# Twelve places for raw weight units, four for split halves, and another order of experts in a one-core decoder layer

## The chip, the core and the metric

The kernel runs on one core of a Trainium2 chip. All times are microseconds (us) on the device. The metric is the time of one execution. Before the change three runs took 1787.58, 1795.78 and 1796.42 us (median 1795.78). Another execution was taken by the hardware profiler: 1789.81 us, of which 1788.0 us lie between its first and its last instruction. All times inside the program are read from that execution, counted from the start of this span.

The engines are named as in the profile: PE is the matrix engine (PEld its weight loads), DVE the vector engine, ACT the scalar engine, POOL the general engine. SP only issues DMAs here; its queue is in order, so a DMA that waits holds back every DMA behind it.

## The reference

One decoder layer on 512 tokens of 1024 channels. The first part (a projection that feeds a causal convolution branch and an mLSTM branch, gates, output projection, layer norm) is not touched by the change. The second part is a mixture of 32 experts of which each token uses four:

```
logits = x2d @ router_w + router_b
top_logit, top_idx = lax.top_k(logits, TOP_K)      # 4 of 32
gate = jax.nn.softmax(top_logit)
...                                                # per expert, on its tokens
h = x[tok] @ w1[e] + b1[e]                         # 1024 -> 2048
g, lin = split(h); g = min(g, 7); lin = clip(lin, -7, 7)
act = g * sigmoid(1.702 * g) * (lin + 1)
y = act @ w2[e] + b2[e]                            # 1024 -> 1024
acc[tok] += w * y
x = layer_norm(ALPHA * x + acc)
```

All weights are 32-bit floats: an expert has 8 MiB of w1 and 4 MiB of w2, 384 MiB in all.

## The kernel before, in words

**Units.** The expert weights lie in memory in *units* of 1 MiB (128 partitions of 2048 floats): eight of w1 and four of w2 for an expert, 384 units in all. `Units.fetch` (line 250) takes the next place of a rotating list, one 8 KiB column of on-chip memory over all partitions, and issues one DMA into it on SP. A place is free again when the last instruction that reads its unit has run. The list (line 1300) has eight places: one of `raw2`, two of `raw`, three of `raw3`, and two of the pool `hl3`, which `Other` lends out as raw places.

**Split or plain.** Experts are ranked by how many tokens they have, and the rank fixes the shape (`RANKS`, line 282): the rows of a block are 128, 64 or 32. Blocks of 64 and 32 rows multiply with the raw unit in plain 32-bit (line 388). Blocks of 128 rows use units that are split into a high and a low half-precision part: `split` (line 270) makes of each half of a unit an ACT copy (line 273) and a DVE subtraction (line 276), into one of six places (two of `hl2`, four of `hl`), and PE runs three passes over them (line 400).

**Kinds of expert.** In the order string `TURNS` (line 293) a letter is a kind: `l` one block of 64 rows, `s` one of 32, `n` 64 and 32, `m` one of 128, `h` 128 and 64 for ranks 1 to 3, and in the kernel before also rank 0, which has two blocks of 128. In front of the string stands `FIRST`, the expert number 0, a block of 128.

**Order of work.** `moe` (line 306) goes through the experts. For the i-th it runs `gemm1` on half 0 of w1 (four units), the first two w2 units of the expert before (`gemm2`), `gemm1` on half 1 (four units), then the last two w2 units of the expert before, and `send` adds the result to the sum `ysum` in memory. So a *block* of work is eight w1 units of expert i and four w2 units of expert i-1. Fetches are issued in this order, as far as places allow. Eight w1 units of `FIRST` are fetched ahead (`ahead`, line 1301). The instruction order on each engine is fixed when the program is built.

**The output biases.** `bias2` (line 1314) adds the gated b2 rows to the token sums `xt` and stores those to `ysum`. It is called at the end of round 0. For each of four token tiles it adds two gate tables, transposes 32 columns, copies, multiplies (line 1332) and adds to `xt`, one tile after the other through a single small buffer. `xt` is the tile `hT` of the profile; after these stores its 16 KiB per partition lie unused until the end, when line 533 loads `ysum` back into it.

Of the kernel before, what the change touches and what calls it, by code (L numbers as in the profile page):

```python
# [23 lines left out]
def f32(ap):  # L24
    return ap.bitcast(F32)
# [74 lines left out]
class Router:  # L100
# [3 lines left out]
    def __init__(self, nc, cp, wp, c, rw, gate, perm):  # L104
        self.nc, self.c, self.rw = nc, c, rw
        self.gate, self.perm = gate, perm

        self.pos1 = cp.tile([P, NT, E], F32, name="pos1")
        self.vals = cp.tile([P, NT, E, 4], F32R, name="vals")
        self.sel = cp.tile([P, E], F32, name="selc")  # L110
        self.selh = cp.tile([P, E], BF, name="selh")
        self.cnt = cp.tile([P, E], F32, name="cnt")
        self.sj = wp.tile([P, NT, TOPK, E], F32, name="sj")
        self.selb = wp.tile([P, NT, 3, E], BF, name="selb")
        self.permf = cp.tile([P, E], F32, name="permf")
# [126 lines left out]
class Units:  # L242


    def __init__(self, nc, raw, hl, pool_share=POOL_HALVES):
        self.nc, self.raws, self.hls = nc, raw, hl
        self.share = pool_share
        self.n = self.f = 0

    def fetch(self, src):  # L250
        w = self.raws[self.f % len(self.raws)].tile([P, 2048], F32, name="raw")
        self.f += 1
        self.nc.sync.dma_start(w, src)
        return w

# [34 lines left out]
    return [(sum(rows[:b]), rows[b]) for b in range(len(rows))]  # L290


TURNS = "lhslmnlhslmlnhslslnmlhslnmlnsll"


def turns():

    kinds = dict(h=[1, 2, 0, 3], m=list(range(4, 8)), n=list(range(8, 13)), l=list(range(13, 25)), s=list(range(25, 31)))
    return [FIRST] + [kinds[k].pop(0) for k in TURNS]


def unit(w, e, *at):
    return w[(e, *at)] if isinstance(e, int) else w[(bass.ds(e, 1), *at)].rearrange("o p n -> p (o n)")


def moe(tc, units, ahead, wr, wq, pp, ph, c, R, x1d, ysum, acc, w1, w2, B1, xg, early, bias2, last, xs, ne=E):

# [72 lines left out]
    def product(xs, outs, w, u, first, end):  # L380

        for x, o in zip(xs, outs):
            if x.dtype == F32:
                m = x.shape[2]
                d = width(m)
                for k in range(2):
                    for j in range(P // m):
                        nc.tensor.matmul(o[j * m:(j + 1) * m], x[:, 2 * u + k, :],  # L388
                                         w[:, k * 1024 + j * d:k * 1024 + (j + 1) * d],
                                         start=first and k == 0, stop=end and k == 1)  # L390
        if all(x.dtype == F32 for x in xs):
# [36 lines left out]
    def swiglu(h, act, half, to):  # L428

        n = act.shape[1]  # L430
        gm = wq.tile([P, F], F32, name="gm", bufs=1)[:, 0:n]
        if half == 0:
            sg = wq.tile([P, F], F32, name="sg", bufs=1)[:, 0:n]
            nc.vector.tensor_scalar(gm, h, LIMIT, None, op0=OP.min)  # L434
            nc.scalar.activation(sg, gm, AF.Sigmoid, scale=SW_ALPHA)  # L435
            nc.vector.scalar_tensor_tensor(act, gm, to[0][:, 0:1], sg, op0=OP.mult, op1=OP.mult)
        else:
            nc.vector.tensor_scalar(gm, h, LIMIT, -LIMIT, op0=OP.min, op1=OP.max)  # L438
            nc.vector.scalar_tensor_tensor(act, gm, 1.0, act, op0=OP.add, op1=OP.mult)
# [8 lines left out]
    def gemm2(ev, half, hs, ys):  # L448

        for u in range(2 * half, 2 * half + 2):  # L450
            product(hs, ys, units.fetch(unit(w2, ev, u)), u, u == 0, u == 3)

    def send(ys, tos):

# [24 lines left out]
    nc.vector.tensor_copy(R.perm, R.permf[0:1])  # L479
    pend = None  # L480
    for i, r in enumerate(seq):
        ev = 0 if r == FIRST else nc.sync.value_load(R.perm[0:1, r:r + 1], min_val=0, max_val=ne - 1)
        more = i + 1 < E
        if i == 0:
            gt, oh = gather(seq[1], 0, False)
            x1 = rows(oh)
            gts = [gather(r, 0, False)[0]]
            for t in range(NT):
                nc.scalar.activation(acc[:, t, :], acc[:, t, :], AF.Copy, scale=ALPHA)
        elif more:  # L490
            gt, g = gather(seq[i + 1], 0)
        acts = [width(m) for m in RANKS[r]]
        if acts[0] == F:
            acts = [wq.tile([P, F], F32, name="act", bufs=2)[:, 0:d] for d in acts]
        else:
            act = wq.tile([P, F], F32, name="act", bufs=2)
            acts = [act[:, i * 512:i * 512 + d] for i, d in enumerate(acts)]
        hold = {}
        for h, act, to in zip(gemm1(r, ev, 0, xs, hold), acts, gts):
            swiglu(h, act, 0, to)  # L500
        if pend is not None:
            pe, pa, pg = pend
# [12 lines left out]
        if pend is not None:
            gemm2(pe, 1, hs, ys)
            if more:
                send(ys, pg)
            else:
                final = [keep(ys[0], pg[0][0])]  # L520
        if i == 0:
            bias2()
        if i == 1:
            early()
        pend = (ev, acts, gts)
        if more:
            gts = gtn
# [685 lines left out]
        return f32(self.pool.tile([P, 2, 1024], F32R, name="hl")).rearrange("p a b -> p (a b)")  # L1213


def body(tc, I, out, ne=E):
    nc = tc.nc
    top = ExitStack()
# [78 lines left out]
        nc.vector.tensor_sub(xs[:, 1, part, :], rows0[g], f32(xs[:, 0, part, :]))  # L1297
    R.order(wp6, pm)

    units = Units(nc, [raw2, raw, raw, raw3, raw3, raw3, Other(hl3), Other(hl3)], [hl2] * 2 + [hl] * 4, set())  # L1300
    ahead = deque(units.fetch(unit(w1, 0, i // 4, i % 4)) for i in range(8))
    nc.scalar.dma_start(posd, R.pos1)
    nc.scalar.dma_start(vald, f32(R.vals))
    nc.gpsimd.memset(xg, 0.0)
# [8 lines left out]

    def bias2():

        b2 = wl.tile([P, D], F32, name="act", bufs=2)[0:E]
        nc.sync.dma_start(b2, I["b2"])
        for n in range(2):
            cols = slice(n * 512, (n + 1) * 512)
            ps = pm.tile([P, 512], F32, name="tp", bufs=2)[0:E]  # L1320
            nc.tensor.matmul(ps, R.sel[0:E, :], b2[:, cols], start=True, stop=True)
            nc.scalar.copy(b2[:, cols], ps)
        for t in range(NT):
            w = wl.tile([P, T], F32, name="gm", bufs=1)
            nc.vector.tensor_add(w[:, 0:E], f32(R.vals[:, t, :, 1]), f32(R.vals[:, t, :, 2]))
            tp = pm.tile([P, 4, P], F32, name="tp", bufs=2)
            nc.tensor.transpose(tp[0:E, 0, :], w[:, 0:E], c["ident"])
            wT = w[0:E, P:2 * P]
            nc.scalar.copy(wT, tp[0:E, 0, :])
            for n in range(2):  # L1330
                ps = pm.tile([P, 512], F32, name="tp", bufs=2)
                nc.tensor.matmul(ps, wT, b2[:, n * 512:(n + 1) * 512], start=True, stop=True)  # L1332
                x = xt[:, t, n * 512:(n + 1) * 512]
                nc.vector.tensor_add(x, ps, x)
# [24 lines left out]
        nc.vector.scalar_tensor_tensor(o, o, r, b, op0=OP.mult, op1=OP.add)  # L1359
        nc.sync.dma_start(out[t * P:(t + 1) * P, :], o)  # L1360

    moe(tc, units, ahead, wr, wl, pm, ph, c, R, x1d, ysum, xt, w1, w2, B1, xg, early, bias2, last, [xs], ne)
    mo.close()

    again = nc.values_load(tabs[0:1, 3, 0:1], min_val=0, max_val=1)
# [41 lines left out]
```

## Time and profile before

| | us |
|---|---|
| median of three runs | 1795.78 |
| the profiled execution | 1789.81 |
| its span | 1788.0 |
| expert stage, from PE's first product of `FIRST` to the last weight unit | 601.7 to about 1745 |
| tail: last sums, layer norm, output | 1743 to 1788 |

PE is busy for 1650.9 us (92%), but a matmul's end is modelled and a wait inside a stretch of short matmuls hardly shows as idle time. The DMA engines' busy share is high in most of the expert stage and falls in a few places; these are in the rows below.

### The profile page before, as it was taken

Reading aid. Unit: us, or ns where it says so; the run is one execution under the profiler, and the core shown is the slowest. Engines: PE = TensorE matmul, PEld = TensorE weight load, DVE = VectorE, ACT = ScalarE, POOL = GpSimd, SP = SyncE. Lnnn points to the kernel's source line nnn. Section 1 sums busy time; section 2 is a strip of 40 time slices with the busy share of each in tenths; the row PEclk is TensorE's granted clock in tenths of the full one; section 3 lists DMA queues with packets and bytes.
Section 4 is the critical chain, followed back from the end, with each engine's and each line's share of the span. In section 5 each row is a group of like instructions: output and inputs, shape, how many; then the busy total and the mean of one; then the engine's idle time right before and its main releaser. Section 6 shows DMA issues by size and latency. Waiting matters only on the chain.

```text
span 1788.0 us, 22808 instructions
## 1 busy us (share of the span) xinstructions
PE 1650.9 (92%) x8848; PEld 1001.8 (56%) x8864; DVE 952.9 (53%) x1423; ACT 554.0 (31%) x731; POOL 228.3 (13%) x169
## 2 busy tenths in 40 slices
PE   7999999899999989989999899998799998999874
PEld 5778878688878836545455453763235553453321
DVE  5999998967567846335353343541125541342013
ACT  4442353434343424223242332421023430231001
POOL 0110031014212001010010301001010102010100
PEclk9999999899999879999999999998999999999997
DMA  5222222122244656999989999689999889999992
GB/s 193 94 71 89 89 94 71 47 95 95 95 157 186 285 205 231 345 394 415 395 327 369 401 414 408 247 315 395 413 412 410 330 325 403 410 408 389 400 419 92
DMA packets 77282, 488.63 MB, mean 273 GB/s; under 512 B 9792, under 2 KB 11600, under 8 KB 22290
## 3 DMA queue, kind: packets, MB, share of 16 engines
q1 hardware_dynamic: 65762, 460.90, 64.5%
q0 software_dynamic: 8960, 19.39, 4.7%
q10 hardware_dynamic: 2448, 6.84, 1.0%
q8 instruction: 71, 1.16, 0.3%
q14 instruction: 41, 0.34, 0.1%
HBM read 471.18 MB, written 19.07 MB: 274 GB/s over the span
## 4 chain that ended last, share of the span: by engine, by line
PE 76%; DMA 13%; DVE 6%; ACT 2%; issue 1%; POOL 0%; SPq 0%; ACTq 0%; DVEq 0%
PE h L388 18%; PE mm L759 18%; PE h L400 13%; DMA raw<-w 10%; PE y L388 7%; PE mm L656 6%; PE y L400 6%; DVE hl L276 2%; DVE acc L816 1%; DMA hT<-ysum 1%; PE tp L366 1%; PE sc L919 1%; PE tp L375 1%; PE h L420 1%; PE tp L1332 1%
## 5 line engine op out<-in xcount | busy, mean ns | idle before, releaser
L276 DVE TENSOR_TENSOR hl<-raw,hl 128x1024 fp32r<-128x1024 f32 x261 | 322.9, 1265 | 130.9 <-ACT hl L273 129.4
L273 ACT CAST hl<-raw 128x1024 fp32r<-128x1024 f32 x261 | 265.0, 1048 | 211.1 <-PE mm L759 75.7
L388 PE MATMUL h<-raw,xs 128*32 128x256 f32 (+1 forms) x2016 | 299.2, 499 | 25.6 <-DMA raw<-w 25.4
L759 PE MATMUL mm<-xhl,hl 128*128 128x512 f32 x1176 | 291.1, 402 | 8.7 <-ACT hl L273 8.7
L400 PE MATMUL h<-hl,xs 128*128 128x512 f32 x1008 | 252.0, 403 | 14.4 <-ACT hl L273 10.0
L759 PEld LDWEIGHTS mm<-xhl,hl 128*128 128x128 f32 x1176 | 224.1, 191 | 64.4 <-ACT hl L273 9.4
L400 PEld LDWEIGHTS h<-hl,xs 128*128 128x128 f32 x1008 | 188.4, 191 | 79.0 <-ACT hl L273 16.1
L388 PEld LDWEIGHTS h<-raw,xs 128*32 128x32 f32 (+1 forms) x2016 | 94.0, 125 | 195.1 <-issue 133.2
L816 DVE SCALAR_TENSOR_TENSOR acc<-zp,vec,acc 128x512 f32<-128x512 f32 x240 | 182.9, 775 | 2.0
L438 DVE TENSOR_SCALAR gm<-h 128x512 f32<-128x512 f32 (+2 forms) x41 | 30.7, 749 | 221.6 <-PE h L388 155.4
L388 PE MATMUL y<-raw,hs 128*64 128x512 f32 (+1 forms) x832 | 128.4, 500 | 6.1 <-DMA raw<-w 4.1
L434 DVE TENSOR_SCALAR gm<-h 128x512 f32<-128x512 f32 (+2 forms) x41 | 30.7, 748 | 193.0 <-PE h L388 161.8
L342 POOL DMA_INDIRECT xg<-x1d,idx x39 | 57.3, 1469 | 540.0 <-DVE oh L325 296.3
L460 POOL DMA_INDIRECT ysum<-yo,idx x39 | 64.6, 1657 | 451.3 <-ACT yo L459 342.3
L400 PE MATMUL y<-hl,hs 128*128 128x512 f32 x432 | 115.1, 410 | 5.6 <-DVE hl L276 2.9
L388 PE MATMUL h<-hl,xs 128*32 128x256 f32 (+1 forms) x672 | 101.0, 492 | 3.6 <-DMA hl<-w 3.3
L400 PEld LDWEIGHTS y<-hl,hs 128*128 128x128 f32 x432 | 78.3, 190 | 37.7 <-issue 10.1
L656 PE MATMUL mm<-hl,xhl 128*128 128x512 f32 x384 | 94.5, 398 | 1.7 <-ACT sg L809 1.5
L388 PEld LDWEIGHTS y<-raw,hs 128*64 128x64 f32 (+1 forms) x832 | 38.5, 124 | 77.8 <-issue 60.0
L656 PEld LDWEIGHTS mm<-hl,xhl 128*128 128x128 f32 x384 | 71.5, 188 | 18.6 <-ACT sg L809 1.8
L459 ACT COPY yo<-y 128x512 f32<-128x512 f32 (+2 forms) x35 | 21.5, 629 | 191.7 <-PE y L388 143.5
L435 ACT ACTIVATE sg<-gm 128x512 f32<-128x512 f32 (+2 forms) x41 | 27.8, 678 | 151.4 <-DVE gm L434 151.3
(308 smaller groups left out, 1576.3 us busy)
## 6 DMA issues: line engine op xcount, KB each, us to landing
raw<-w SPq DMA_DIRECT2D x288, 1024.0 KB, 12.2
hl<-w SPq DMA_DIRECT2D x96, 1024.0 KB, 11.3
raw<-wf SPq DMA_DIRECT2D x44, 1024.0 KB, 4.8
cvp<-xT SPq DMA_DIRECT2D x8, 256.0 KB, 5.4
hT<-x SPq DMA_DIRECT2D x1, 2048.0 KB
x1d<-hT ACTq DMA_DIRECT2D x4, 512.0 KB, 6.3
ysum<-hT ACTq DMA_DIRECT2D x4, 512.0 KB, 2.6
hT<-ysum SPq DMA_DIRECT2D x1, 2048.0 KB, 22.4
```

Source lines behind the costliest of these rows:

```text
L273: nc.scalar.copy(s[:, 0, :], w)
L276: eng.tensor_sub(s[:, 1, :], w, f32(s[:, 0, :]))
L342: nc.gpsimd.indirect_dma_start(out=g, out_offset=None, in_=split_rows(x1d, m), in_offset=bass.IndirectOffsetOnAxis(ap=ix[:, 0:1], axis=0), ...
L388: nc.tensor.matmul(o[j * m:(j + 1) * m], x[:, 2 * u + k, :], w[:, k * 1024 + j * d:k * 1024 + (j + 1) * d], start=first and k == 0, stop=e ...
L400: nc.tensor.matmul(o[:, j, :], x[:, a, 2 * u + k, :], s[k][:, b, j * 512:(j + 1) * 512], start=first and k == 0 and i == 0, stop=end and k ...
L434: nc.vector.tensor_scalar(gm, h, LIMIT, None, op0=OP.min)
L435: nc.scalar.activation(sg, gm, AF.Sigmoid, scale=SW_ALPHA)
L438: nc.vector.tensor_scalar(gm, h, LIMIT, -LIMIT, op0=OP.min, op1=OP.max)
L460: nc.gpsimd.indirect_dma_start(out=split_rows(ysum, P * d // D), out_offset=bass.IndirectOffsetOnAxis(ap=ix[:, 0:1], axis=0), in_=o, in_of ...
L656: nc.tensor.matmul(ps, src[:, a, kk, t * P:(t + 1) * P], w[k][:, b, :], start=(kk == 0 and (a, b) == PASS[0]), stop=(kk == KD - 1 and (a, ...
L759: nc.tensor.matmul(ps, w[k][:, a, j * P:(j + 1) * P], mov[:, b, k, :], start=(k == 0 and (a, b) == PASS[0]), stop=(k == KD - 1 and (a, b) ...
L816: nc.vector.scalar_tensor_tensor(o, z[:, j:j + T], V("dw_w", m * CT + j), o, op0=OP.mult, op1=OP.add)
```

## The change

Five edits:

- The places for raw units are ten from the start: `raw2`, two of `raw`, three of `raw3`, two of `hl3`, two of `hl2`. Once `bias2` has stored `xt`, the method `also` adds its two 8 KiB slices in front of the list: twelve. Before round 30 (`i == E - 2`) the slices are taken out again, since `xt` is loaded at the end.
- The split halves have four places (`hl`) instead of six.
- Two w2 units of `FIRST` are fetched ahead with its eight w1 units (`ahead2`).
- `bias2` runs between the two halves of round 0's first-layer work and the next expert, and its products run on four groups of 32 rows: one transpose for all four token tiles, and the four tiles' products each on its own group of rows and into its own bank.
- The order string is another, and rank 0 has a letter of its own, `H`.

```diff
-        self.nc, self.raws, self.hls = nc, raw, hl
+        self.nc, self.raws, self.hls = nc, deque(raw), hl
...
+    def also(self, places):
+        self.raws.extend(p for p in places)
+        self.raws.rotate(len(places))
+        self.raws = deque(p for p in self.raws if not isinstance(p, Slice) or p in places)
...
-        w = self.raws[self.f % len(self.raws)].tile([P, 2048], F32, name="raw")
-        self.f += 1
+        w = self.raws[0].tile([P, 2048], F32, name="raw")
+        self.raws.rotate(-1)
...
-TURNS = "lhslmnlhslmlnhslslnmlhslnmlnsll"
+TURNS = "lnllmlshlsHslmshlllnlmnnnmshsll"
...
-            product(hs, ys, units.fetch(unit(w2, ev, u)), u, u == 0, u == 3)
+            w = ahead2.popleft() if ahead2 else units.fetch(unit(w2, ev, u))
+            product(hs, ys, w, u, u == 0, u == 3)
...
+        if i == E - 2:
+            units.also([])
...
+        if i == 0:
+            bias2()
         if pend is not None:
...
-        if i == 0:
-            bias2()
...
+class Slice:
+    def __init__(self, ap):
+        self.ap = ap
+    def tile(self, *_, **__):
+        return self.ap
...
-    units = Units(nc, [raw2, raw, raw, raw3, raw3, raw3, Other(hl3), Other(hl3)], [hl2] * 2 + [hl] * 4, set())
+    units = Units(nc, [raw2, raw, raw] + [raw3] * 3 + [Other(hl3)] * 2 + [Other(hl2)] * 2, [hl] * 4, set())
     ahead = deque(units.fetch(unit(w1, 0, i // 4, i % 4)) for i in range(8))
+    ahead2 = deque(units.fetch(unit(w2, 0, i)) for i in range(2))
...
+        for n in range(2):
+            cols = slice(n * 512, (n + 1) * 512)
+            y = pm.tile([P, 2, 512], F32, name="y", bufs=1)
+            sums = [y[:, 0, :], y[:, 1, :]] + [pm.tile([P, 512], F32, name="tp", bufs=2) for _ in range(2)]
+            for t in range(NT):
+                part = slice(t * E, (t + 1) * E)
+                nc.tensor.matmul(sums[t], wT[part], p2[part, cols], start=True, stop=True)
+            for t in range(NT):
+                nc.vector.tensor_add(xt[:, t, cols], sums[t], xt[:, t, cols])
         for t in range(NT):
...
             nc.scalar.dma_start(ysum[t * P:(t + 1) * P], xt[:, t, :])
+        units.also([Slice(xt[:, 2 * k:2 * k + 2, :].rearrange("p a b -> p (a b)")) for k in range(2)])
```

The instruction order moves at three places. First, SP's queue where the expert stage begins; `raw<-w` and `hl<-w` are fetches, `TENSOR_LOAD perm` reads an expert's number, of which there are 31. Before:

```order
L253 DMA raw<-w 128x2048
L253 DMA hl<-w 128x2048 x2
L253 DMA raw<-w 128x2048 x3
L482 TENSOR_LOAD perm
L482 ISA x2
L253 ISA
L253 DMA raw<-w 128x2048
```

After, at the same place:

```order
L259 DMA raw<-w 128x2048
L259 DMA hl<-w 128x2048 x4
L259 DMA raw<-w 128x2048 x3
L491 TENSOR_LOAD perm
L491 ISA x2
```

Two more fetches stand ahead of the expert numbers. The fetches that before stood between the numbers are gone from there. SP's queue goes on, after the last two numbers, with the first fetches into `xt` (`hT<-w`):

```order
L491 TENSOR_LOAD perm
L491 ISA x2
L259 DMA hl<-w 128x2048
L259 ISA
L259 DMA hT<-w 128x2048
L259 ISA
L259 DMA hT<-w 128x2048
L259 ISA
```

Behind these two stand all the next fetches into the six `raw` places, which in the kernel before were issued as each came free.

Second, PE around `bias2`; L1321 and L1344 gather the b2 rows by rank, L1327 and L1350 transpose the gates, L1332 and L1359 are the products, L400 and L406 the split products of `FIRST`. Before:

```order
L420 LDWEIGHTS selh
L420 MATMUL h<-B_3618,selh 128x512
L1321 MATMUL tp<-act,selc 32x512 x2
L1327 MATMUL tp<-ident,gm 32x128
L1332 MATMUL tp<-act,gm 128x512 x2
L1327 MATMUL tp<-ident,gm 32x128
L1332 MATMUL tp<-act,gm 128x512 x2
```

After:

```order
L406 MATMUL h<-hl,xs 128x512 x12
L1344 MATMUL tp<-yo,gm 128x512 x2
L1350 MATMUL tp<-ident,gm 128x128
L1359 MATMUL y<-yo,gm 128x512 x2
L1359 MATMUL tp<-yo,gm 128x512 x2
L1359 MATMUL y<-yo,gm 128x512 x2
L1359 MATMUL tp<-yo,gm 128x512 x2
L336 MATMUL tp<-vals,oh 128x4 x4
```

It now follows the last product of `FIRST`'s first layer directly, with one transpose instead of four, while before the first half of the next expert's w1 came ahead of it.

Third, PE where rank 0 begins. The rows `y<-` are the w2 products of the expert before it, with the rows of that expert's blocks (64x512, 32x256). Before:

```order
L388 MATMUL y<-raw,hs_7524 64x512 x4
L400 MATMUL h<-hl,xs 128x512 x26
L375 MATMUL tp<-ident,xg 128x128 x8
L400 MATMUL h<-hl,xs 128x512 x14
L330 MATMUL tp<-vals,oh 128x4 x4
L400 MATMUL h<-hl,xs 128x512 x56
L366 MATMUL tp<-ident,act 128x128 x6
```

After:

```order
L394 MATMUL y<-hl,hs_6538 64x512 x8
L381 MATMUL tp<-ident,xg 128x128 x8
L336 MATMUL tp<-vals,oh 128x4 x4
L406 MATMUL h<-hl,xs 128x512 x24
L381 MATMUL tp<-ident,xg 128x128 x8
L406 MATMUL h<-hl,xs 128x512 x4
L336 MATMUL tp<-vals,oh 128x4 x4
L406 MATMUL h<-hl,xs 128x512 x20
L372 MATMUL tp<-ident,act 128x128 x2
L406 MATMUL h<-hl,xs 128x512 x48
L394 MATMUL y<-raw,hs_6836 32x256 x16
```

Rank 0 now stands between two `s` experts, whose w2 products (32x256) lie in its first layer; before, it followed an `n` expert.

## Rows read from the trace of the kernel before

**Rows 1.** The page: engines, and the span in 40 slices.

```profile
PE 1650.9 (92%) x8848; PEld 1001.8 (56%) x8864; DVE 952.9 (53%) x1423; ACT 554.0 (31%) x731; POOL 228.3 (13%) x169
PEclk9999999899999879999999999998999999999997
DMA  5222222122244656999989999689999889999992
```

**Rows 2.** Stretches: length, busy us of each engine, granted clock, DMA share, GB/s.

```profile
602.00:650.00 48.00, 45.30 (x222) 30.07 (x222) 30.44 (x43) 24.80 (x27) 0.00 (x0) 0.95 0.80 316
650.00:720.00 70.00, 65.81 (x254) 36.86 (x256) 44.11 (x71) 26.21 (x32) 6.77 (x13) 0.84 0.57 187
920.00:945.00 25.00, 25.00 (x113) 13.34 (x114) 11.28 (x13) 7.04 (x9) 1.95 (x2) 1.00 0.61 219
1120.00:1180.00 60.00, 60.00 (x362) 42.34 (x366) 33.32 (x38) 21.01 (x25) 3.08 (x3) 1.00 0.57 222
1405.00:1460.00 55.00, 54.93 (x311) 29.65 (x310) 31.75 (x35) 21.60 (x26) 6.48 (x4) 1.00 0.76 276
1460.00:1743.00 283.00, 250.66 (x1643) 107.17 (x1642) 74.00 (x123) 51.48 (x74) 30.81 (x20) 0.99 1.02 405
1743.00:1788.00 45.00, 20.60 (x64) 6.70 (x60) 16.02 (x24) 4.54 (x5) 2.22 (x4) 0.78 0.24 94
```

**Rows 3.** What SP's queue waited for: total us, times, longest.

```profile
SPq L253 <- DVE hl L276: 598.6, 99, 31.8
SPq L253 <- PE h L388: 474.5, 193, 29.0
```

**Rows 4.** DMA issues between 720 and 1743: count, size, median us to landing.

```profile
raw<-w SPq DMA_DIRECT2D x263, 1024.0 KB, 13.3
hl<-w SPq DMA_DIRECT2D x88, 1024.0 KB, 13.0
```

**Rows 5.** PE in order of time (start, us): four, two and four units' products.

```profile
692.04 11.32 PE L400 MATMUL h<-hl,xs 128*128 128x512 f32 x48
704.71 3.65 PE L388 MATMUL h<-raw,xs 128*64 128x512 f32 x16
740.15 3.63 PE L388 MATMUL h<-raw,xs 128*32 128x256 f32 x64
```

**Rows 6.** PE at the starts of blocks 5, 8, 14 and 16.

```profile
799.46 11.90 PE L400 MATMUL h<-hl,xs 128*128 128x512 f32 x38 [3.14 <-ACT hl L273]
904.75 0.70 PE L400 MATMUL h<-hl,xs 128*128 128x512 f32 x2
...
1116.84 0.74 PE L400 MATMUL h<-hl,xs 128*128 128x512 f32 x2 [1.63 <-ACT hl L273]
1210.10 0.50 PE L330 MATMUL tp<-vals,oh 128*128 128x4 f32 x4
```

**Rows 7.** The end of `FIRST`'s first layer, and the output biases.

```profile
629.70 2.56 PE L400 MATMUL h<-hl,xs 128*128 128x512 f32 x10
643.52 2.30 PE L1321 MATMUL tp<-act,selc 32*32 32x512 f32 x4 [2.20 <-DMA act<-b]
663.07 3.78 PE L1332 MATMUL tp<-act,gm 32*128 32x512 f32 x4 [0.40 <-ACT gm L1329]
666.88 0.69 DVE L1334 TENSOR_TENSOR hT<-tp,hT 128x512 f32<-128x512 f32 x1 [1.01 <-PE tp L1332]
```

**Rows 8.** Stores to `ysum` (median us to landing), and the reads of the expert numbers.

```profile
ysum<-hT ACTq DMA_DIRECT2D x4, 512.0 KB, 2.6
...
L482 SPq TENSOR_LOAD <-perm x31: 260/269/466, 603.5 to 626.3; - x31
```

**Rows 9.** What the split's ACT copy (L273) waited for between 602 and 1743.

```profile
  DMA raw<-w: 71.1, 24
  PE h L400: 28.5, 36
```

**Rows 10.** The page: the split's two instructions, count, busy us, mean ns.

```profile
L276 DVE TENSOR_TENSOR hl<-raw,hl 128x1024 fp32r<-128x1024 f32 x261 | 322.9, 1265 | 130.9 <-ACT hl L273 129.4
L273 ACT CAST hl<-raw 128x1024 fp32r<-128x1024 f32 x261 | 265.0, 1048 | 211.1 <-PE mm L759 75.7
```

More of the change, by code (lines that the diff above doesn't have):

```diff
@@ L245, in __init__ @@
     def __init__(self, nc, raw, hl, pool_share=POOL_HALVES):
-        self.nc, self.raws, self.hls = nc, raw, hl
+        self.nc, self.raws, self.hls = nc, deque(raw), hl
         self.share = pool_share
-        self.n = self.f = 0
+        self.n = 0
+    def also(self, places):
+        self.raws.extend(p for p in places)
+        self.raws.rotate(len(places))
+        self.raws = deque(p for p in self.raws if not isinstance(p, Slice) or p in places)
     def fetch(self, src):
-        w = self.raws[self.f % len(self.raws)].tile([P, 2048], F32, name="raw")
-        self.f += 1
+        w = self.raws[0].tile([P, 2048], F32, name="raw")
+        self.raws.rotate(-1)
         self.nc.sync.dma_start(w, src)
@@ L290, in blocks @@
     return [(sum(rows[:b]), rows[b]) for b in range(len(rows))]
-TURNS = "lhslmnlhslmlnhslslnmlhslnmlnsll"
+TURNS = "lnllmlshlsHslmshlllnlmnnnmshsll"
 def turns():
-    kinds = dict(h=[1, 2, 0, 3], m=list(range(4, 8)), n=list(range(8, 13)), l=list(range(13, 25)), s=list(range(25, 31)))
+    kinds = dict(h=[1, 2, 3], m=list(range(4, 8)), n=list(range(8, 13)), l=list(range(13, 25)), s=list(range(25, 31)), H=[0])
     return [FIRST] + [kinds[k].pop(0) for k in TURNS]
@@ L303, in unit, with moe @@
     return w[(e, *at)] if isinstance(e, int) else w[(bass.ds(e, 1), *at)].rearrange("o p n -> p (o n)")
-def moe(tc, units, ahead, wr, wq, pp, ph, c, R, x1d, ysum, acc, w1, w2, B1, xg, early, bias2, last, xs, ne=E):
+def moe(tc, units, ahead, ahead2, wr, wq, pp, ph, c, R, x1d, ysum, acc, w1, w2, B1, xg, early, bias2, last, xs, ne=E):
     nc = tc.nc
@@ L1314, in bias2 @@
     def bias2():
-        b2 = wl.tile([P, D], F32, name="act", bufs=2)[0:E]
-        nc.sync.dma_start(b2, I["b2"])
+        b2, p2 = (wl.tile([P, D], F32, name="yo", bufs=2) for _ in range(2))
+        nc.sync.dma_start(b2[0:E], I["b2"])
+        w = wl.tile([P, F], F32, name="gm", bufs=1)
+        sel = w[0:E, 2 * P:3 * P]
+        nc.vector.tensor_copy(sel.rearrange("p (t e) -> p t e", t=NT), R.sel[0:E, None, :].to_broadcast([E, NT, E]))
         for n in range(2):
             cols = slice(n * 512, (n + 1) * 512)
-            ps = pm.tile([P, 512], F32, name="tp", bufs=2)[0:E]
-            nc.tensor.matmul(ps, R.sel[0:E, :], b2[:, cols], start=True, stop=True)
-            nc.scalar.copy(b2[:, cols], ps)
@@ L1323, in bias2 @@
-        for t in range(NT):
[L1324 to L1334, printed above, removed]
+            ps = pm.tile([P, 512], F32, name="tp", bufs=2)
@@ new lines, in bias2 @@
+            nc.tensor.matmul(ps, sel, b2[0:E, cols], start=True, stop=True)
+            nc.scalar.copy(p2[:, cols], ps)
+        nc.vector.tensor_add(w[:, 0:P].rearrange("p (t e) -> p t e", t=NT), f32(R.vals[:, :, :, 1]),
+                             f32(R.vals[:, :, :, 2]))
+        ps = pm.tile([P, 512], F32, name="tp", bufs=2)
+        nc.tensor.transpose(ps[:, 0:P], w[:, 0:P], c["ident"])
+        wT = w[:, P:2 * P]
+        nc.scalar.copy(wT, ps[:, 0:P])
+        for n in range(2):
[7 more added lines that the diff above has]
+                nc.vector.tensor_add(xt[:, t, cols], sums[t], xt[:, t, cols])
@@ L1360, in last @@
         nc.sync.dma_start(out[t * P:(t + 1) * P, :], o)
-    moe(tc, units, ahead, wr, wl, pm, ph, c, R, x1d, ysum, xt, w1, w2, B1, xg, early, bias2, last, [xs], ne)
+    moe(tc, units, ahead, ahead2, wr, wl, pm, ph, c, R, x1d, ysum, xt, w1, w2, B1, xg, early, bias2, last, [xs], ne)
     mo.close()
```

## The prediction

> **What bounds the kernel now.** I read the page first, then a table of stretches, then what SP's queue waits for. The page has PE at 92% [rows 1], which looks like the bound; but the line of the DMA engines stands at nine tenths from slice 17 on and falls only in a few slices. In the long stretch 1460 to 1743 its share is 1.02 at 405 GB/s [rows 2]: there the stream of weights is the bound, and PE takes each unit as it lands. The share is lower in three holes: 920 to 945 (0.61), 1120 to 1180 (0.57), 1405 to 1460 (0.76) [rows 2]. The missing shares are 0.39 x 25 + 0.43 x 60 + 0.24 x 55 = 9.8 + 25.8 + 13.2 = 48.8 us. In these PE is busy for the whole stretch: the experts with a block of 128 rows beside another take PE longer than their weights take to load, all eight places hold unread units, and SP's fetches wait for readers [rows 3]. A fourth loss is the start, 602 to 720: 0.20 x 48 + 0.43 x 70 = 39.7 us idle [rows 2].
>
> The price of a unit in a full stream: between 720 and 1743 SP issued 263 + 88 = 351 units [rows 4] in 1023 - 48.8 = 974.2 us of flowing stream, so 2.77 us a unit, the gathers and scatters included, and 33.2 us for a block of twelve. By 720 therefore 384 - 351 = 33 units had been issued; I count 32 as landed.
>
> The Trainium skill ("DMA: Bandwidth & Descriptors", Specifications) gives about 358 GB/s as the HBM limit of a core. By it a unit would cost 2.77 x 405 / 358 = 3.13 us and the coming stream could not be as fast as I say. The 405 GB/s over 283 us contradict it here, so the row stands.
>
> **The start.** Ten units are fetched before 602 instead of eight. The last two w2 units of FIRST go into places that its own w1 units leave, behind the 31 expert numbers (0.27 us each and two short instructions, from 603.5 to 626.3 in the row with fetches between [rows 8]), so at about 625. Then the queue stops: the next fetch is into hT and must wait until bias2 has stored it, and six free raw places wait behind it. When is that? FIRST's first layer ends at 629.70 + 2.56 = 632.3 [rows 7], and bias2 follows directly on PE. Before, it took from 643.5 to 667.6 [rows 7], 24 us, one token tile after the other. Now: two gather products (2.3 us at most [rows 7]), a copy, one transpose, then twice four products on four row groups with four DVE additions of 0.69 us each behind them. With the groups side by side that is about 2.3 + 1.5 + 2 x (1.0 + 2.8) = 11.4 us, the last addition at 643.7, and a store lands 2.6 us later [rows 8]: 646. If the groups ran one after the other, a set of four would cost about 7.6 us, twice the 3.78 of the row with two products [rows 7], at the clock of that stretch (0.84 on average [rows 2]), and the gate would open near 659. No row shows row groups side by side; I take the lower value, since the column groups in rows 5 do overlap (a unit of 64 rows costs PE less than a split one), and keep 659 as an end of the range. An earlier opening than 641 I exclude: eight additions alone are 5.5 us after 635.
>
> The Trainium skill ("TensorE: Matmul & The Clock Gate", Part 3) lists a measured 3.07 for four row groups of K=32 and N=512. By it a set of four costs 7.6 / 3.07 = 2.5 us instead of 1.0, and the gate opens 3 us later, at 649. No run here shows it yet.
>
> So at 646 twelve units have landed, where the stream before was further, and from there it is never short of places in the first blocks. By 720 it has 12 + 74 / 2.77 = 38.7 units instead of 32. The 372 units after the gate end the stream, if nothing interrupts it, at 646 + 372 x 2.77 = **1676.4**. Before, the same reading gives 720 + 352 x 2.77 = 1695 without its holes.
>
> **The holes.** PE's price of a unit [rows 5]: split 11.32 / 4 = 2.83; 64 rows 3.65 / 2, less the overlap of neighbours, 1.80; 32 rows 3.63 / 4 = 0.91. So m costs 2.83, l 1.80, s 0.91, n 2.71, h 4.63, H 5.66. A block costs eight of its own, four of the expert before, and an allowance for biases, transposes and waits. Blocks 5 to 7 (m, n, l) ran from 799.5 to 904.8 [rows 6]: 105.3 us for 87.9 us of units, so 5.8 a block, some waiting in it. Blocks 14 and 15 (H, s) ran from 1116.8 to 1210.1 [rows 6]: 93.3 for 86.0, so 3.7 a block. These are my two ends.
>
> I walk through the new order with a lead of the stream that grows by PE's price less 33.2, never falls below 0, and stops at twelve places (33.2 us); what would go beyond is a hole. With 5.8: block 8 (h) costs 46.5 and the lead is 13; block 9, l and h's w2, 38.7, lead 19; s takes it back to 6; H costs 54.7, lead 27; block 12, s and H's w2, 35.7, lead 30; l, m, s bring it to 14; h and the l behind it to 33.0, just under the limit; three lights to 21; then n l m n n n m: leads 29 and 33, holes of 0.7, 5.1 and 6.1; the last h a hole of 4.5; s, l, l leave a lead of 16.4. So 16.4 us of holes and, since the lead at the end is work that PE still has when the last unit lands, a lag of 16.4: together 33. With 3.7 the same walk has no hole and no lag. Checked on the kernel before (eight places, lead 8 at block 5), 5.8 gives 32 us where the trace has 48.8, with H at its right place; so I take the upper end, **33**, and for the range let 6.5 stand, which gives 43 before and 31 + 18.5 = 50 after. Rank 0's hole is the one that goes by the order: two light experts empty the lead ahead of it. The four further places give the other 11 us a hole.
>
> **The four split places.** The split now runs at most two units ahead. In m experts its ACT copy waited 71.1 us for weights and 28.5 for a place [rows 9], so places are seldom what it lacks. A place's turn is copy 1.05, subtraction 1.27 [rows 10] and PE's 2.83 / 2 = 1.42, 3.7 in all; four places come round in 4 x 1.42 = 5.7: covered, cost 0. If a swiglu step of DVE falls between, PE may lose a few us in each of ten experts with 128 rows, which lies in the 6.5 above. ACT, DVE, POOL have the same work otherwise.
>
> **The sum.** 1676.4 + 33 + tail 45 [rows 2] + 1.8 outside the span = 1756.2, against 1789.8 in the profiled execution: 34 less. The tail stays: the same two l experts end, and hT is free by then. The profiled execution stands at the lower of the runs (1787.6; the others 1795.8 and 1796.4), so I add 2 for a median: **1758**.
>
> **Rivals.**
> - *The stream never fills.* Allowance 3.7: 1676.4 + 45 + 1.8 = 1723. For it: the H stretch itself; PE's clock falls less when it waits less. Against: the holes before, which 3.7 makes only 8 us.
> - *PE becomes the bound.* Allowance 6.5 and the gate at 656: 1773 + 10 = 1783. For it: PE is fully busy in the holes, and n n n m in a row has no light expert.
> - *No change:* the gate opens near 680 and eats both gains, 1756 + 34 = 1790.
> - *Slower.* One mechanism: hT is a gate in SP's in-order queue, and all fetches wait behind it. Each us after 646 is a us of idle stream. From 690 on the kernel is slower than before, at 700 it takes 1810. For it: the load of b2 now goes into a tile that waits for the tables of the router, and in the changed order it stands behind 19 of the expert numbers; bias2 can't start without it. Against: the numbers end by 626, and even the old 24 us after 632 plus a store end at 659.
>
> **How the numbers follow.** The forecast has 0.50 (1738 to 1772), no holes 0.20 (1723 to 1738), PE bound 0.17 (1772 to 1787), no change 0.08, slower 0.05. About 0.5% is what a measurement here tells from no change: faster means under 1786.8. The first three give 0.87. The range 1728 to 1788 leaves out half of the second case, the slower one and some of the fourth, near 0.2.
>
> **What would show it.** Right: the first hT fetch issued at 641 to 659 and none of the raw fetches before it; DMA share 1.0 from there for at least 300 us; the hole at rank 0 under 10 us; a lead at the end seen as PE working without waits for weights in the last two experts. Wrong: a share under 0.7 for 20 us or more in the first 400 us after the gate, PE waiting for split halves in m experts, or the gate after 665.

## The result, and the profile after

The changed kernel takes 1771.22 us (median of 4 runs, 1768.74 to 1773.01) where the kernel before takes 1793.07: a ratio of 0.9865, 95% interval 0.9835 to 0.9895. It is faster by 1.35%, 22 us; forecast were 1758 us and 34 us less. The profiled execution took 1768.74 us, its span 1766.7; before, 1789.81 and 1788.0. One run of the kernel e2 below took 2312.86 us at a granted clock of 0.67 and is left out of its figures.

The page, with the lines that answer to [rows 1]:

```profile
PE 1628.9 (92%) x8861; PEld 1011.7 (57%) x8861; DVE 957.4 (54%) x1421; ACT 558.2 (32%) x728; POOL 229.8 (13%) x169
PEclk9999999899999979999899999999999999999997
DMA  5222222122244549999979989989999998998992
```

PE is as busy as before, in share. The DMA line stands at 4 to 5 in slices 12 to 15, is full for five, and then has a dent every few slices. The stretches show them. Columns: length, busy us of PE, PEld, DVE, ACT and POOL, granted clock, DMA share, GB/s.

```profile
602.00:651.00 49.00, 42.49 (x207) 30.48 (x207) 37.48 (x60) 25.38 (x27) 0.19 (x1) 0.85 0.23 81
651.00:880.00 229.00, 204.64 (x1144) 92.78 (x1144) 71.12 (x115) 49.92 (x66) 26.21 (x24) 0.96 1.02 403
885.00:915.00 30.00, 26.13 (x109) 19.34 (x109) 17.99 (x21) 12.77 (x13) 1.59 (x2) 0.93 0.65 258
1035.00:1055.00 20.00, 19.72 (x160) 13.63 (x162) 12.88 (x16) 6.32 (x9) 3.49 (x2) 1.00 0.71 266
1175.00:1195.00 20.00, 16.92 (x70) 12.01 (x71) 12.06 (x14) 9.73 (x10) 1.05 (x1) 0.91 0.60 241
1420.00:1515.00 95.00, 92.54 (x805) 44.00 (x802) 27.27 (x56) 17.33 (x27) 10.12 (x8) 1.00 0.90 354
1590.00:1612.00 22.00, 18.47 (x77) 14.27 (x75) 13.72 (x12) 9.97 (x11) 2.33 (x1) 0.92 0.75 257
1612.00:1724.00 112.00, 100.06 (x646) 39.93 (x645) 27.51 (x46) 18.29 (x28) 10.58 (x7) 1.00 0.99 394
```

Against [rows 2]: the start is a gap of 49 us (share 0.23) and then the stream flows at 1.02 for 229 us, where it had flowed at 0.57 up to 720. The hole at rank 0 (before 1120 to 1180, 25.8 us; now 1035 to 1055) has shrunk to 0.29 x 20 = 5.8 us. But the h experts still have theirs (885, 1175, 1590; before, two of the three holes of [rows 2], at 920 and 1405, stood at h experts too), with four more places, and a new one stands in the row of n experts (1420 to 1515).

SP's queue at the gate and at the first of these holes (start, us; a long DMA row is one that waited), and what it waited for between 883 and 920 (total us, times, longest):

```profile
622.63 7.19 SPq L259 DMA_DIRECT2D hl<-w  x2
650.95 3.16 SPq L259 DMA_DIRECT2D hT<-w  x2
654.30 3.13 SPq L259 DMA_DIRECT2D raw<-w  x6
...
882.62 33.92 SPq L259 DMA_DIRECT2D hl<-w  x4
...
SPq L259 <- PE h L394: 28.6, 3, 26.3
```

At 622 to 630 come the two w2 units that were forecast, then nothing until 650.95, when the first fetch into `xt` goes out and six fetches into free places follow at once. From 888.2 a fetch waits for 26.3 us, until 914.5. PE in that stretch runs an h expert (a block of 128 rows: L406; a block of 64: L394):

```profile
881.86 12.33 PE L406 MATMUL h<-hl,xs 128*128 128x512 f32 x46 [1.62 <-DVE hl L282]
...
899.05 12.35 PE L406 MATMUL h<-hl,xs 128*128 128x512 f32 x46 [0.79 <-DVE hl L282]
911.23 0.60 PE L372 MATMUL tp<-ident,xg 128*128 128x128 f32 x4
...
912.51 3.65 PE L394 MATMUL h<-hl,xs 128*64 128x512 f32 x16 [0.33 <-ACT xs L373]
915.99 3.60 PE L394 MATMUL h<-hT,xs 128*64 128x512 f32 x16
```

The first block goes through all eight w1 units before the second block's tokens are even transposed (911.23); only from 912.51 on are the units read a second time, and the first place comes free at 914.5. Eight of twelve places are held for over 30 us. The same kind of expert in the kernel before:

```profile
911.59 1.66 PE L400 MATMUL h<-hl,xs 128*128 128x512 f32 x6
913.18 1.94 PE L388 MATMUL h<-hl,xs 128*64 128x512 f32 x8
915.05 5.28 PE L400 MATMUL h<-hl,xs 128*128 128x512 f32 x22
920.26 1.94 PE L388 MATMUL h<-hl,xs 128*64 128x512 f32 x8
```

There the two blocks alternate, and a unit is done with soon after its first product. In the changed kernel the written order of PE has all three h experts and four of the five n experts with one block behind the other.

### The profile page after: what moved, and what is told of

The parts are those of the page before. It is cut to its first block, busy times and chain, and to the rows that moved or that the text cites. A ratio compares the mean times of both kernels' runs of the same rounds, so it can differ in the third digit from the quotient of the medians.

```text
span 1766.7 us, 22869 instructions
## 1 busy us (share of the span) xinstructions
PE 1628.9 (92%) x8861; PEld 1011.7 (57%) x8861; DVE 957.4 (54%) x1421; ACT 558.2 (32%) x728; POOL 229.8 (13%) x169
## 4 chain that ended last, share of the span: by engine, by line
PE 70%; DMA 19%; DVE 7%; ACT 2%; issue 1%; POOL 0%; SPq 0%; ACTq 0%; POOLq 0%; DVEq 0%
PE mm L768 17%; PE h L394 15%; PE h L406 11%; DMA raw<-w 9%; PE mm L665 7%; DMA hl<-w 6%; PE y L394 6%; PE y L406 5%; DVE hl L282 2%; DVE acc L825 1%; DMA hT<-ysum 1%; PE tp L372 1%; PE h L426 1%; PE sc L928 1%; DMA raw<-wf 1%
## 5 line engine op out<-in xcount | busy, mean ns | idle before, releaser
L282 DVE TENSOR_TENSOR hl<-raw,hl 128x1024 fp32r<-128x1024 f32 x197 | 247.0, 1273 | 94.9 <-ACT hl L279 93.3
L279 ACT CAST hl<-raw 128x1024 fp32r<-128x1024 f32 x197 | 202.9, 1047 | 206.1 <-PE mm L768 75.6
L406 PE MATMUL h<-hl,xs 128*128 128x512 f32 x1008 | 253.3, 405 | 12.0 <-DVE hl L282 7.0
L406 PEld LDWEIGHTS h<-hl,xs 128*128 128x128 f32 x1008 | 190.3, 193 | 69.6 <-DVE hl L282 11.9
L394 PE MATMUL h<-raw,xs 128*32 128x256 f32 (+1 forms) x1360 | 202.6, 501 | 18.1 <-DMA raw<-w 18.1
L394 PEld LDWEIGHTS h<-raw,xs 128*32 128x32 f32 (+1 forms) x1360 | 68.4, 125 | 133.5 <-issue 85.8
L406 PE MATMUL y<-hl,hs 128*128 128x512 f32 x432 | 115.6, 413 | 5.4 <-ACT hl L279 3.1
L467 POOL DMA_INDIRECT ysum<-yo,idx x39 | 71.9, 1843 | 348.3 <-ACT yo L466 160.1
L282 DVE TENSOR_TENSOR hl<-hl 128x1024 fp32r<-128x1024 f32 x76 | 90.5, 1222 | 46.2 <-ACT hl L279 45.5
L394 PE MATMUL h<-hl,xs 128*32 128x256 f32 (+1 forms) x688 | 98.6, 487 | 4.8 <-DMA hl<-w 2.5
L394 PE MATMUL y<-raw,hs 128*32 128x256 f32 (+1 forms) x656 | 96.6, 486 | 6.3 <-DMA raw<-w 4.3
L406 PEld LDWEIGHTS y<-hl,hs 128*128 128x128 f32 x432 | 79.9, 193 | 38.7 <-issue 12.8
L279 ACT CAST hl<-hl 128x1024 fp32r<-128x1024 f32 x76 | 77.7, 1052 | 67.7 <-DMA hl<-w 31.5
L394 PE MATMUL h<-hT,xs 128*32 128x256 f32 (+1 forms) x640 | 86.9, 476 | 1.5 <-DMA hT<-w 1.5
L394 PE MATMUL y<-hl,hs 128*32 128x256 f32 (+1 forms) x592 | 82.7, 477 | 0.4 <-DMA hl<-w 0.4
## 6 DMA issues: line engine op xcount, KB each, us to landing
hl<-w SPq DMA_DIRECT2D x128, 1024.0 KB, 20.4
```

The lines of the kernel that those rows point to most:

```text
L279: nc.scalar.copy(s[:, 0, :], w)
L282: eng.tensor_sub(s[:, 1, :], w, f32(s[:, 0, :]))
L394: nc.tensor.matmul(o[j * m:(j + 1) * m], x[:, 2 * u + k, :], w[:, k * 1024 + j * d:k * 1024 + (j + 1) * d], start=first and k == 0, stop=e ...
L467: nc.gpsimd.indirect_dma_start(out=split_rows(ysum, P * d // D), out_offset=bass.IndirectOffsetOnAxis(ap=ix[:, 0:1], axis=0), in_=o, in_of ...
```

## The experiments

"Units by 720" are those landed in the profiled execution, "idle" is the DMA engines' idle time from 720 to the last weight packet, against the 1.02 of a full stretch, and "last" is when that packet landed; all three are counted in the trace's DMA records, the idle time to about 1 us. Ratios are to the kernel before, with 95% intervals. The kernel before was run beside each group and took 1794.67 us beside e1 to e4, 1792.88 beside e5 to e8 and 1796.34 beside e9 to e12, so kernels of different groups are compared by their ratios.

| kernel | us | ratio | units by 720 | idle | last |
|---|---|---|---|---|---|
| before | 1793.07 | | 31.1 | 55.5 | 1744.7 |
| changed | 1771.22 | 0.9865 (0.9835 to 0.9895) | 36.1 | 50.1 | 1723.5 |
| e1 second block early | 1774.29 | 0.9884 (0.9864 to 0.9904) | 37.1 | 50.8 | 1724.8 |
| e2 old string | 1797.32 | 1.0013 (0.9992 to 1.0033) | 35.1 | 79.4 | 1754.3 |
| e3 string alone | 1774.30 | 0.9883 (0.9864 to 0.9902) | 32.0 | 40.3 | 1727.3 |
| e4 ten places | 1766.95 | 0.9837 (0.9808 to 0.9866) | 39.3 | 57.6 | 1722.2 |
| e5 four halves | 1773.27 | 0.9899 (0.9877 to 0.9921) | 35.0 | 43.8 | 1725.3 |
| e6 slices last | 1768.56 | 0.9867 (0.9843 to 0.9891) | 39.7 | 61.6 | 1725.1 |
| e7 e6, all second blocks early | 1747.45 | 0.9740 (0.9717 to 0.9763) | 42.4 | 44.5 | 1700.8 |
| e8 e7, six halves, ten places | 1761.61 | 0.9812 (0.9787 to 0.9836) | 37.9 | 38.9 | 1718.6 |
| e9 e6, H's second block early | 1758.39 | 0.9791 (0.9770 to 0.9813) | 39.7 | 51.9 | 1715.4 |
| e10 e6, those of h and n early | 1761.19 | 0.9807 (0.9785 to 0.9829) | 41.2 | 58.1 | 1721.8 |
| e11 slices first, all early | 1766.71 | 0.9841 (0.9821 to 0.9860) | 36.0 | 45.7 | 1724.0 |
| e12 e7, old string | 1746.14 | 0.9711 (0.9688 to 0.9733) | 40.0 | 34.4 | 1700.8 |

The table adds up: from before to changed, 5.0 more units by 720 at 2.74 us are 13.7, the idle is 5.4 less, and the flow between gives the rest of the 21.2 us by which the last packet comes earlier.

**e1: the second block's tokens gathered early.**

```diff
-    xg = wr.tile([P, D], F32, name="xg")
+    xg = wr.tile([P, D + 512], F32, name="xg")
...
             gt, g = gather(seq[i + 1], 0)
+            two = [gather(seq[i + 1], b, off=width(blocks(seq[i + 1])[0][1])) for b in range(1, len(blocks(seq[i + 1]))) if seq[i + 1]]
...
-                gt, g = gather(seq[i + 1], b)
+                gt, g = two[b - 1] if seq[i + 1] else gather(seq[i + 1], b)
```

> One edit of the changed kernel: the tokens of an expert's second block (h: 64 rows, n: 32 rows) are gathered together with those of its first block, into columns of their own, and not after the first block's transposes. In the written order PE's products of the two blocks then alternate unit by unit in all three h and all five n experts (H stays). Theory A, held units: the 48 us of idle stream between 660 and 1700 come from experts whose second block starts only after the first block has gone through all eight w1 units, so that eight of twelve places stay occupied for some 30 us. Then the idle stream falls to 10 to 20 us (H's 6.5 stays), and the time to 1735 to 1752. Theory B, PE's price: these blocks simply cost PE 55 us where I allowed 46, in whatever order; then the h blocks keep 55 us or more, the idle stream stays over 40 us, and the time at 1766 to 1775.

Of theory A only the holes of the h experts came true, of theory B the time (1774.29) and the sum of the idle (50.8). PE now alternates, at the same place:

```profile
878.87 1.65 PE L406 MATMUL h<-hl,xs 128*128 128x512 f32 x6
880.46 1.94 PE L394 MATMUL h<-hl,xs 128*64 128x512 f32 x8
882.32 3.06 PE L406 MATMUL h<-hl,xs 128*128 128x512 f32 x12
```

In the blocks of the three h experts (from one expert's last swiglu to the next one's) the idle stream falls from 11.2 + 8.7 + 9.3 = 29.2 us to 0.2 + 1.0 + 0.0. So the held units did make these holes. But the sum of the idle time stays (50.8), since H (13.9 where it had 6.5) and the stretch n, n, n, m, s (31 where it had 11) take it over, and the time is unchanged. A hole is filled, and the stream runs into full places one heavy expert later: theory A explains where the holes stood, not what they cost.

The longest of the new holes, 18 us in the m and the s, is a held place too, but not of a second block. SP waits 29.5 us there for w2 units of the last n expert (first row: SP's waits between 1520 and 1560). They are fetched ahead of the last four w1 units of the m, but PE goes through all eight w1 units of the m, from 1517 to 1548, before its first product with a w2 unit at 1553.94:

```profile
SPq L259 <- PE y L394: 31.3, 2, 29.5
...
1534.97 13.22 PE L406 MATMUL h<-hl,xs 128*128 128x512 f32 x46 [0.30 <-DVE hl L282]
...
1553.94 2.29 PE L394 MATMUL y<-raw,hs 128*64 128x512 f32 x12
```

The longest wait of this kind is 7.8 us in the changed kernel at this place; in e7 and e11, below, it is 29.7 and 28.4.

**e2, e3: the order of experts apart.** e2 is the changed kernel with `TURNS = "lhslmnlhslmlnHslslnmlhslnmlnsll"`; e3 is the kernel before with the changed string.

> The changed kernel with the order of experts of before (rank 0 at its old place, after an n). By the walk of the prediction (5.8 us a block, twelve places) the order is worth nothing: 18 us of holes and lag against 33 with the new one, so about 1756. By theory A every two-block expert holds its eight units in either order, and rank 0 begins with a lead that its n has left behind: a hole of 15 to 25 us at rank 0, and 1775 to 1790.

> The kernel before with the new order of experts alone: eight places, six split halves, the biases late. The walk gives 28 us of holes and a lag of 5 against 32, so no change: 1788 to 1796. If the new order is what removes the 25 us hole at rank 0 without giving it back elsewhere, 1765 to 1775. By theory A nothing is held here, since with eight places the blocks mostly alternate in the written order: the sum of holes is set by PE, 1785 to 1800.

e3 alone gives 20 of the 22 us, and e2 none: by itself all the rest of the change is worth nothing with the old order. For e3 that is the second of its three cases; e2 lies above the range of theory A too. In e3 the idle falls by 15 us and the hole at rank 0 from 26 us [rows 2] to 9 (0.37 x 25):

```profile
1025.00:1050.00 25.00, 25.00 (x194) 18.51 (x193) 13.23 (x15) 8.20 (x11) 3.69 (x2) 1.00 0.63 247
```

The walk, which saw no value in the order, is wrong for both; the sentence of the prediction on rank 0's hole is right. From e3 to the changed kernel 4.1 more units land by 720 (11 us), and the idle after it grows by 9.8: the early start is given back.

**e4, e6: the gate taken away.** e4 leaves out the call of `also`; e6 leaves out its `rotate`, so that the slices stand behind the other places.

> The changed kernel without the two slices of xt: ten places throughout, and nothing on SP's queue waits for the biases. Two things change against the changed kernel: the stream can start before 651 (worth up to 25 us), and the places are ten. By the walk ten places lose the same 33 us as twelve, so the time falls by the earlier start, to 1750. By theory A eight held units leave two places to run ahead where the blocks don't alternate, and the holes grow by 2 units x 2.75 us at each such expert, some 5 us x 6 = 30 us: about 1775, the earlier start given back.

> The changed kernel with the two slices of xt behind the other ten places in the list, not in front: the fetches between 625 and 651 go into places that the first expert leaves, and nothing waits for the biases until two fetches into the slices come round. By the prediction's start (a us of gate is a us of stream) the stream flows some 20 us earlier and the time falls to 1751 to 1756. If PE is the bound from block 8 on, the earlier stream only fills the places sooner: the idle stream after 720 grows by what is won before, as in e4 (26.9 + 57.6 us against 38.5 + 50.1), and the time is 1764 to 1771.

Both start earlier (3.2 and 3.6 units more by 720, 9 to 10 us), and both lose it again (idle 57.6 and 61.6 for 50.1). e4 lands between its two theories, and its 4 us are not clear of noise (0.9837, interval up to 0.9866). For e6 the second holds: opening the gate alone is worth nothing that can be told, 0.9867 against 0.9865.

**e5: four places for split halves.** e3 with `[hl] * 4` where it had `[hl2] * 2 + [hl] * 4`.

> e3 (the kernel before with the new order alone, 1774.3) with four places for split halves and not six; the two places of hl2 lie unused, and PE's written order is nearly that of e3. The prediction priced four places at 0: then 1772 to 1777 and 37 to 43 us of idle stream after 720. The rival: what the changed kernel loses in its middle (its stream idles 50 us after 720, where e3's idles 40) comes from PE waiting for halves in the blocks of 128 rows, since fewer halves can be made ahead; then 1780 to 1786, and idle near 50.

1773.27 for 1774.30, or by the ratios 0.9899 for 0.9883: they cost nothing that can be told, as priced. The idle is 43.8, just over the range for this case. Three more units land by 720 than in e3, so it is the time, and not the middle alone, that stays.

**e7, e8: both edits together.** e7 is e6 with the edit of e1, extended to H (`xg` of `2 * D`). e8 is e7 with `[hl2] * 2 + [hl] * 4` for halves and eight places and the slices for raw units.

> The changed kernel with three edits: slices last (as in the run before this one), the second block's tokens gathered with the first's (as in e1), and that for H too, whose second block waited 3.4 us for its gather. If what e1 lost again in its later blocks came from H's gather and the late start, 1745 to 1758. If PE's own work is the bound whatever the start and the order within an expert, 1764 to 1772.

> As e7, but hl2 stays with the split halves: six places for halves, ten for raw units (eight and the two slices). If four halves cost PE time in blocks of 128 rows, this is the fastest of all, 1740 to 1755, and below e7 by 8 us or more. If they cost nothing, it equals e7 within 4 us, or is slower by the holes of two places less (5 to 10 us).

e7 takes 24 us off the changed kernel, 22 by the ratios (0.9740 for 0.9865). Its edits one by one take off nothing that can be told: slices last 0.9867 (e6), all second blocks early 0.9841 (e11, below), with intervals that overlap that of the changed kernel. e8 is 14 us slower than e7, which neither of its cases had: two places are worth more than two halves. The loss is not in idle time after 720, which is less than e7's. It starts later (4.5 units by 720, 12 us; until the biases it has eight raw places where e7 has ten), and the rest is a slower flow (2.77 us a unit against 2.74, 10 us over its 346 units) whose cause is open. What e7 no longer has is seen in H. In e6 PE waits there for gathered tokens twice:

```profile
985.54 1.77 PE L380 MATMUL tp<-ident,xg 128*128 128x128 f32 x8 [3.27 <-DMA xg<-x1d,idx]
...
1000.41 0.66 PE L371 MATMUL tp<-ident,xg 128*128 128x128 f32 x2 [4.97 <-DMA xg<-x1d,idx]
```

and in e7 at the same work not at all:

```profile
974.73 1.03 PE L380 MATMUL tp<-ident,xg 128*128 128x128 f32 x8
...
1019.84 0.38 PE L371 MATMUL tp<-ident,xg 128*128 128x128 f32 x2
```

PE's waits for gathers between 660 and 1730 are 6.3 us in the changed kernel, 8.2 in e1, 15.4 in e6 and none in e7; H's block lasts 71.6, 75.3, 78.7 and 62.8 us.

**e9 to e12: e7 taken apart.** e9 is e6 with only H's second block early, e10 e6 with only those of h and n, e11 e7 with the slices in front again, e12 e7 with the old string.

> e6 (slices last, 1768.6) with only H's second block gathered early; h and n keep one block behind the other. Theory C: from block 8 on PE sets the end, and e7 won 21 us over e6 because PE no longer waits for gathers (15 us between 660 and 1730 in e6, none in e7) and because the two blocks of h and n alternate. Here only the first falls away: 1755 to 1763. If the gathers are all of it, 1745 to 1752; if the alternation is all of it, 1766 to 1771.

> e6 with the second blocks of h and n gathered early and H's not: the other half of e7. By theory C 1755 to 1763; 1745 to 1752 if the alternation is all of e7's gain, 1766 to 1771 if H's gather is all of it.

> The changed kernel with the second blocks of h, n and H gathered early, and the slices of xt in front as in the changed kernel, so that SP still waits for the biases until 651. Theory C: with nothing left that PE waits for in the middle, the start counts in full: block 7 ends some 15 us later than in e7, so 1758 to 1766. If the stream's start is no part of it, 1745 to 1751.

> e7 with the old order of experts. Theory C: PE has the same work in any order, so with an early start and alternating blocks the order is worth little: 1747 to 1757. If the order itself is the gain (20 us between before and e3, 26 between e2 and the changed kernel), 1765 to 1775.

From e6 (0.9867), H alone takes off 0.76% (e9, 13 to 14 us), h and n alone 0.60% (e10, 11 us), both 1.27% (e7, 23 us): neither is all of it, and within the noise the two add up. e11 shows that the start then counts: 19 us between it and e7, for 6.4 units (17.5 us) by 720. And in e12 the order, worth 26 us between e2 and the changed kernel, is worth nothing that can be told: 0.9711 for 0.9740, with the last packet at 1700.8 in both. Yet rank 0's block has its hole again in e12, 67 us at a share of 0.69, or 22 us of idle:

```profile
1089.00:1156.00 67.00, 65.27 (x372) 44.95 (x372) 36.95 (x40) 27.25 (x32) 5.46 (x3) 1.00 0.69 262
```

So whether a hole stands at rank 0 does not decide the time. Theory C had e9 and e10 in their ranges, e12 a little too high (1747 to 1757) and e11 a little too low (1758 to 1766).

## Why the prediction was right, and where it was wrong

The time lay in the range and the direction was right; the point was 13 us too low. That the time came so near is in part luck: of the 34 us of the sum, 19 were to come from the earlier start (1695 to 1676.4) and 16 from a smaller loss behind it (48.8 to 33), and the walk gave the order nothing. By e3 the order alone makes 20 of the measured 22, and by e2 the rest without it makes none. For the profiled execution the sum said 1756.2 and it took 1768.74. Term by term:

- *The gate, 646.* It opened at 650.95: +5. `bias2`'s first copy stood behind splits and a swiglu on DVE and ran at 636.0, not 632; from there on it took 12.6 us to the last addition where I had 11.4, and the store 2.4.

```profile
636.33 3.32 PE L1344 MATMUL tp<-yo,gm 32*128 32x512 f32 x4 [2.57 <-issue]
640.49 1.22 PE L1359 MATMUL y<-yo,gm 32*128 32x512 f32 x2 [0.44 <-ACT gm L1352]
640.50 1.22 PE L1359 MATMUL tp<-yo,gm 32*128 32x512 f32 x2
641.50 1.06 PE L1359 MATMUL y<-yo,gm 32*128 32x512 f32 x2
641.52 1.06 PE L1359 MATMUL tp<-yo,gm 32*128 32x512 f32 x2
...
647.29 1.28 DVE L1361 TENSOR_TENSOR hT<-tp,hT 128x512 f32<-128x512 f32 x2
```

The groups do run side by side: four products in 2.1 us (640.49 to 642.58), where the row with two took 3.78 [rows 7], at a granted clock of 0.50, the lower level (1.2 GHz), in both (changed kernel, then before; the clock is the third figure from the end):

```profile
640.40:642.70 2.30, 2.09 (x8) 0.52 (x8) 0.09 (x1) 0.04 (x1) 0.00 (x0) 0.50 0.00 0
...
663.00:667.00 4.00, 3.93 (x5) 1.38 (x6) 0.81 (x2) 0.02 (x1) 0.00 (x0) 0.50 0.31 124
```

I had taken 1.0, and 0.84, the average of 650 to 720, for the clock of that row. The prediction's estimate from the Trainium skill ("TensorE: Matmul & The Clock Gate", Part 3) was 2.5, nearer to what was measured.

- *The flow, 372 units at 2.77.* From 651 to 1723.5 less 50.4 us of idle are 1022.1, 2.748 a unit: -8. The 403 GB/s of 651 to 880 bear the row out, against the 358 that the prediction cites from the Trainium skill ("DMA: Bandwidth & Descriptors", Specifications).

- *Holes and lag, 33.* Measured 50.4 of idle and 2.4 from the last packet to PE's last product at 1726.0: +20. **This is the term that was mis-sized**, and the step behind it is the limit of the walk, a lead that "stops at twelve places (33.2 us)"; with it fails the sentence that "the four further places give the other 11 us a hole". The walk frees a unit as PE reads it. In the changed kernel a unit of a two-block expert is read twice, some 30 us apart (PE's rows at 881.86 and 912.51, SP's wait of 26.3 us until 914.5), so the twelve places hold four units ahead there, not twelve. The first hole came at block 8, where the walk had a lead of 13 us and no hole. The holes are 34 us more than the walk's 16.4, and of its lead of 16.4 at the end 2.4 are left: the two errors cancel in part. From e3 to the changed kernel, which is all of the change but the order, the idle grew by 10 us. The order of the blocks stood in PE's written order, which I read at three places, and an h expert was not among them.

  PE's pace between was as priced. Blocks 8 to 29 took 780.7 us, waits included, and their units cost 650.8 at the prices of the prediction: 5.9 a block more, where the walk had 5.8. What it missed most comes behind them. By the walk block 8 begins without a lead at 646 + 80 x 2.77 = 867.6, block 29 ends at 867.6 + 650.8 + 22 x 5.8 = 1646, and PE's last product 63 us later, with weights landed ahead; measured were 1652.8 and 73.2 us later, with PE waiting for a stream at 1.02:

```profile
872.10:1652.80 780.70, 736.18 (x4648) 402.50 (x4650) 336.22 (x451) 244.09 (x303) 93.43 (x59) 0.98 0.95 378
1652.80:1726.00 73.20, 63.32 (x326) 22.23 (x325) 11.01 (x20) 6.34 (x11) 5.82 (x4) 1.00 1.02 407
```

  How much of the 20 us the held places make is not shown: e1 frees those of the h experts, and the time stays.

- *The tail, 45.* From PE's last product 40.7: -4. The work in it has not changed: from the last weight packet to the end it is 43.2, before 43.3. No lag was left since s, l, l ran out of lead: between 1652.8 and 1726.0 PE waits eleven times for weights, 6.9 us in all.

The sum is +5 - 8 + 20 - 4, the 12.5 that were missing but for rounding.

**The order.** Right where the prediction spoke of rank 0's hole (e3: 26 to 9 us), wrong in its walk, which gave the new string the same loss as the old one.

**What a us of gate is worth.** I had equated them. e6 and e4 open the gate and gain nothing, or 4 us that are not clear of noise; e11 to e7, the same edit with the second blocks early, gains 19. Block 8 begins at 872.1 in the changed kernel, at 859.4 in e6 and at 853.0 in e7, and blocks 8 to 29 take 780.7, 794.7 and 778.3 us. So e6 loses in the middle what it won before, and e7 keeps it:

```profile
859.40:1654.10 794.70, 741.86 (x4635) 407.04 (x4649) 336.19 (x451) 244.35 (x303) 93.42 (x59) 0.97 0.94 372
```

An early stream paid only where PE did not lose the time again.

**The marks that I named.** The first fetch into `xt` between 641 and 659: right. Share 1.0 for 300 us: wrong, it held for 229. Rank 0 under 10 us: right, 5.8. A lead at the end: wrong. A share under 0.7 for 20 us in the first 400 us: it came, at 885 to 915 (0.65), and it was the sign that the walk was off. The other two signs did not come: PE's waits for split halves in all experts between 660 and 1730 are 16.5 us where they were 19.5, and the gate opened before 665.

**The rivals.** PE as the bound (1783) came in kind, not by its allowance of 6.5: in the changed kernel it was 5.9, in e7 (778.3 us for the same blocks) 5.8. These two, and e12 beside e7 (two orders, one end), speak for the work of PE with its hand-offs as what sets the pace there. It is argued: no run makes PE's work itself shorter. e7:

```profile
853.00:1631.30 778.30, 745.39 (x4629) 394.07 (x4642) 330.19 (x446) 243.03 (x303) 99.04 (x58) 0.99 0.96 380
1631.30:1701.00 69.70, 60.57 (x318) 21.87 (x317) 13.42 (x22) 6.21 (x11) 5.89 (x4) 1.00 1.02 407
```

In e7 PE is busy 96% up to 1631 and the stream 0.96; the last experts are bound by the stream again. How much of PE's busy time is hidden waiting inside matmuls the trace does not show, so how far this is from PE's own limit stays open. Open too is what H's gather is worth at a late start: e11, with H added, has 0.9841 where e1 has 0.9884, 8 us, and the intervals just part, but against the changed kernel (0.9865) neither is clear of noise, and I ran no kernel with H alone and a late start.

## What to carry to other kernels

A buffer counts by how long its slowest reader keeps it: before pricing more places, look in the written order for data that is read twice, or read later than what was fetched behind it, and for the distance in time. When stream and engine are both nearly full, a remedy alone may only move the idle time; test them together, as here two edits gave nothing that could be told apiece (e6, e11) and 24 us in e7. An order of work that is worth 26 us (e2 to the changed kernel) may be worth nothing once the stream starts early and the gathers are early (e7 to e12).

## What the runs showed of the hardware

- Four products of K = 32 and N = 512 in 32-bit floats on four row groups took 2.1 us where two one after the other took 3.78, 3.6 times the rate, at a granted clock of 0.50 in both.
- With twelve places instead of eight a fetch took longer from issue to landing, and a gather hardly. In the changed kernel (issues from 720 to 1700: count, size, median us to landing) a weight unit takes 17.5 to 20.4 us where it took about 13 [rows 4], a gather of tokens 8.0, and in the kernel before 7.5:

```profile
raw<-w SPq DMA_DIRECT2D x172, 1024.0 KB, 17.5
hl<-w SPq DMA_DIRECT2D x116, 1024.0 KB, 20.4
hT<-w SPq DMA_DIRECT2D x52, 1024.0 KB, 18.0
...
xg<-x1d,idx POOLq DMA_INDIRECT x35, 8.0
```
